# Weight halves at other places in their buffers, and two other orders of the queries' matmuls

## The chip, the cores and the metric

The kernel runs on one core of a Trainium2 chip. The metric is the device time of one execution in microseconds. A profiled execution has a span besides, from its first to its last instruction, and all positions below are microseconds from the start of that span.

## The reference, cut to what matters

Two decoder layers over 256 tokens of width 2048, in f32. The first is a Mamba-2 mixer: one wide projection of the modulated input, a causal convolution, a chunked scan, a gate, and a projection back. Then one shared K and V is made for three head groups of dilated attention, and the second layer attends with queries of its own.

```
h = x*(1+scale)+shift                      # modulation from c
z, xBC, dt = split(h @ in_w)               # 2048 x 10304
xBC = silu(causal_conv(xBC))               # xs (4096), B (1024), C (1024)
y = ssd_scan(xs*dt, dt*A, B, C) + D*xs;  y = rms(y*silu(z)) @ out_w
x = layer_norm(alpha*x + (1+gate)*y)
k, v = split(x @ kv_w)                     # 2048 x 6144, shared
q, z = split(h2 @ in_w2)                   # 2048 x 4096
o = merge(three dilated windows of softmax(q k) v) * silu(z)
out = layer_norm(alpha*x + (1+gate)*(o @ out_w2))
```

## The kernel before, in words

Nearly all work is matrix products with 256 tokens. Every f32 operand is held as two fp32r halves, a high half (`hi`, a rounded copy) and a low half (`lo`, the rest), and a product is made of hi by hi, hi by lo and lo by hi. A product is accumulated over 16 k-tiles of 128 rows of the contraction.

Weights come in pieces of 128 x 1024 f32 (512 KB). SyncE's queue loads each into `raw`; ScalarE copies it to `whi` (line 100), VectorE subtracts to get `wlo` (line 102). Both halves lie in buffers of 1088 elements per partition, four for each half, used in turn, so a piece of 1024 may start at any of the first 65 elements: `halves_at(off)` places hi at `off[0]` and lo at `off[1]`, in elements of 4 bytes. Two places are used: `SHORT = (16, 16)` and `LONG = (0, 0)`. The buffers themselves start at multiples of 256 bytes, and so does the activation tile `actT`.

There are three kinds of product:

- `tm_chunk` (lines 213 to 215): the activations are the loaded weights of TensorE (the stationary operand) and the weight halves stream past, 512 columns at a time. Their halves lie at LONG.
- `cm_quad` and `cm_piece` (lines 151 to 153): the weight halves are stationary, 128 x 128, and 256 columns of activations stream past. Their halves lie at SHORT. After the start of the kernel it makes the products for B and C, called `bc`, of groups 2, 4 and 6.
- `cm_wide` (lines 182 and 185), the wide products: the weight halves are stationary here too. For each k-tile four matmuls run: the two high halves (n = 0, 1) against 512 columns (activations hi and lo side by side, line 182), then the two low halves against 256 columns (activations hi, line 185). A call has 16 k-tiles in 4 pieces. There are 12 calls for xs (groups 2 to 7, two each, 256 to 483 us), 12 for K (766 to 899 us), 12 for the queries (two half sets `hq`, 965 to 1032 us, and 1034 to 1117 us among the first attention) and 4 for the second gate.

Below, a long matmul is one of 512 columns and a short one is one of 256 columns.

The order on TensorE follows the program's text nearly everywhere; the framework's scheduler interleaves the independent work of attention with the products. The next product's first piece is begun ahead (`begin_next`, `upcoming`), with the place given there by `firsts` or by the lists of the K products; this place has to be the same that the product itself uses.

Of the kernel before, what the change touches and what calls it, by code (L numbers as in the profile page):

```python
# [18 lines left out]
P = 128  # L19
L = 256  # L20
D = 2048
KT = D // P
# [5 lines left out]
NG = 3  # L28
# [21 lines left out]
def trunk(ctx, tc, xT, x, c, par, cst, bias, lnrow, ada, wdt, win, wxs, wout, wk, wv, wbin, wbout, out):  # L50
    nc = tc.nc
    V, S, T, PO = nc.vector, nc.scalar, nc.tensor, nc.gpsimd
# [27 lines left out]
    ones = cc[:, CM:CM + 128]  # L80
    cons.tile([P, 32], F32, name="pad")
    SHORT, LONG = (16, 16), (0, 0)

    def rows(t, b):

        return t.rearrange("(j r) n -> r j n", r=2)[b]
# [19 lines left out]
    upcoming, ready, owed = [], [], []  # L106
# [7 lines left out]
    def first_or(src, q, off=(0, 0)):  # L114

        return ready.pop() if ready else split(load_piece(src[q]), off=off)
# [38 lines left out]
    def acc_pair(pool=None):  # L155
        return [(pool or mm).tile([P, 2, L], F32, name="acc") for _ in range(2)]

    def cm_quad(src, ahi, alo, rate=(0, 1), k0=0):
        ps = acc_pair()
        for q in range(k0 // 2, KT // 2):  # L160
            w = first_or(src, q, SHORT)
            if q == KT // 2 - 1:
                begin_next()
            cm_piece(src, q, ps, ahi, alo, k0=k0, w=w)
            background(*rate)
        return ps

    def cm_wide(src, dst, rate=(0, 1), moving=None, later=False):

        both, high = moving or (lambda kt: xp[:, kt], lambda kt: xhi[:, kt, :])  # L170
        ps = acc_pair()
        for q in range(KT // 4):
            w = first_or(src, q, SHORT)
            if q == 1:
                settle()
            if q == KT // 4 - 1:
                begin_next()
            hi, lo = (t.rearrange("p k n -> p (k n)").rearrange("p (k n) -> p k n", k=4) for t in w)
            for k in range(4):
                kt = 4 * q + k  # L180
                for n in range(2):
                    T.matmul(ps[n], hi[:, k, n * P:n * P + P], both(kt), start=kt == 0, stop=False,  # L182
                             skip_group_check=True)
                for n in range(2):
                    T.matmul(ps[n][:, 0, :], lo[:, k, n * P:n * P + P], high(kt), start=False, stop=kt == KT - 1,  # L185
                             skip_group_check=True)
            background(*rate)
        def put():
            for n in range(2):
                S.activation(dst[:, n, :], ps[n][:, 1, :], AF.Copy)  # L190
                V.tensor_tensor(dst[:, n, :], ps[n][:, 0, :], dst[:, n, :], op=ALU.add)

        if later:
            owed.append(put)
        else:
            with behind_next():
                put()
# [125 lines left out]
    def drain():  # L323
        while jobs:
            jobs.pop(0)()


    hp = act.tile([P, 2, KT, L], F32R, name="actT")
    hhi, hlo = hp[:, 0], hp[:, 1]
# [4 lines left out]
    with ExitStack() as cA:  # L334
# [15 lines left out]
        with ExitStack() as cS:  # L350
# [8 lines left out]
            xs, bc, sz = {}, {}, dict(enumerate(szt))  # L359
# [29 lines left out]
            def xs_wide(g):  # L389

                xs[g] = pxs.tile([P, 4, L], F32, name="xs")
                for w in range(2):
                    t = xs[g][:, 2 * w:2 * w + 2, :]
                    cm_wide(wxs[2 * g - 4 + w], t, rate=R, moving=(lambda kt: hp[:, :, kt, :], hh_))
                    for n in range(2):
                        conv(t[:, n, :], 4 * g + 2 * w + n, t[:, n, :])

            def product(kind, g, pre=None):

                if kind == "xs" and g > 1:  # L400
                    return xs_wide(g)

                src, k0, part = begun.get((kind, g), (None, 0, None))
                if src is None:
                    src = win[{"bc": g // 2, "xs": 4 + g, "z": 6 + g}[kind]]
                if kind == "z":
                    ps = tm_chunk(src, hh_, hl_, rate=R, k0=k0, pre=pre)
                    if g not in sz:
                        sz[g] = p0.tile([P, 2, 512], F32, name="sz")
                    with behind_next():  # L410
                        for b in range(2):
                            if part is not None:
                                V.tensor_tensor(part[:, b, :], ps[b], part[:, b, :], op=ALU.add)
                            S.activation(sz[g][:, b, :], part[:, b, :] if part is not None else ps[b], AF.Silu)
                    return
                ps = cm_quad(src, hhi, hlo, rate=R, k0=k0)
                t = tiles(ps)
                if part is not None:
                    with behind_next():
                        for w in range(2):  # L420
                            V.tensor_tensor(part[:, 2 * w:2 * w + 2, :], ps[w], part[:, 2 * w:2 * w + 2, :],
                                            op=ALU.add)
                    t = [part[:, n, :] for n in range(4)]
                if kind == "xs":
                    xs_conv(g, t)
                else:
                    bc_conv(g, t)

            with ExitStack() as c0:
# [83 lines left out]
                for row in ("b4:0. b6:0. h z2:0. z1:0. b2:0 x1:0 h", "b2:1. x1:1. z1:1. z4:0 h h",  # L513
# [123 lines left out]
                for i, (k, q, ends) in enumerate(order):  # L637
# [7 lines left out]
                    for j in (i, i + 1):  # L645
                        if j < len(order) and j not in halves and order[j][0] != "dt":
                            with tc.issue_after(highs[j // 2 - 1]) if j in (7, 9) else ExitStack():
                                halves[j] = split(pieces[j], after=dots[0] if j == 5 else None,
                                                  off=LONG if str(order[j][0])[0] == "z" else SHORT)
# [5 lines left out]
                    z = str(k)[0] == "z"  # L655
# [3 lines left out]
                    k0, k1 = (begin[k], 2 * q + 2 if ends else KT) if k in part else (0, KT)  # L659
# [18 lines left out]
            aux2 = cS.enter_context(tc.tile_pool(name="aux2", bufs=2, space=PSUM, reuse_waits="tile"))  # L678
            px = pe = cS.enter_context(tc.tile_pool(name="px", bufs=2, reuse_waits="tile"))
            R = (1, 10)  # L680


            scratch = wp1.tile([P, D], F32, name="araw")
# [104 lines left out]

            def firsts(kind, g):
                if kind == "xs" and g > 1:  # L790
                    return [(wxs[2 * g - 4 + w], 0, SHORT) for w in range(2)]
                src, k0, _ = begun.get((kind, g), (None, 0, None))
                if src is None:
                    src = win[{"bc": g // 2, "xs": 4 + g, "z": 6 + g}[kind]]
                return [(src, k0 // 2, LONG if kind == "z" else SHORT)]

            for g in range(G - 1):
                for kind in ("bc",) * (g % 2) + ("xs", "z"):
# [108 lines left out]
        for n in range(4):  # L907
            ps = tm_chunk(wout[n], lambda kt: y_to(kt)[0], lambda kt: y_to(kt)[1],
                          nk=2 * KT, rate=(1, 4) if n else (1, 2),
                          pre={0: y_ahead, 3: first_weights}.get(n), split_end=4 if n == 3 else 0)  # L910
# [55 lines left out]
    kv, vt = {}, {}  # L966
# [11 lines left out]
    with ExitStack() as cL:  # L978
# [34 lines left out]
        for q in range(2, KT // 2):  # L1013
# [3 lines left out]
            for j in range(2):  # L1017
                with tc.issue_after(end.ins):
                    w = split(load_piece(wv[2 * j][q]), after=tile4.ins if q == 2 else None)
# [3 lines left out]

        R = (1, 2)
        pin[0] = latest[-1].ins
        with tc.issue_after(tile4.ins):
            state[0] = 0
            queue(pl, cols1[11:])
            jobs.append(lambda: gate_out(1))
            upcoming.extend((wk[2 * (2 * g + hq) + w], 0, SHORT) for hq in range(2) for g in range(NG) for w in range(2))  # L1030
            upcoming.extend((wv[1 + 2 * g], 0, LONG) for g in range(NG))
            evict_v(0, 2, tm_chunk(wv[4], hx, lx, rate=R))
            for hq in range(2):
                for g in range(NG):
                    kv[hq, g] = place(3 + 3 * hq + g, [P, 4, L])
                    for w in range(2):
                        cm_wide(wk[2 * (2 * g + hq) + w], kv[hq, g][:, 2 * w:2 * w + 2, :], rate=R, later=True)
            for g in range(NG):
                evict_v(1, g, tm_chunk(wv[1 + 2 * g], hx, lx, rate=R))
            drain()  # L1040
            late = latest[-1].ins

        ada_bias(1, slice(0, KT), slice(0, 2))
        for kt in range(KT):
            t = pl.tile([P, L], F32, name="htmp")
# [10 lines left out]
    R = (0, 1)  # L1056
# [22 lines left out]
    def queries(hq):  # L1079
        qq = [pc2.tile([P, 4, L], F32, name=f"q{g}") for g in range(NG)]  # L1080
        upcoming.extend([(wbin[2 * (2 * g + hq) + w], 0, SHORT) for g in range(NG) for w in range(2)][1:])
        for g in range(NG):
            for w in range(2):
                cm_wide(wbin[2 * (2 * g + hq) + w], qq[g][:, 2 * w:2 * w + 2, :], rate=(1, 1),
                        later=(g, w) != (NG - 1, 1))
        return qq

    def attend(hq, qq):
# [98 lines left out]
    for n in range(2):  # L1187
        ps = tm_chunk(wbout[n], *og, nk=H)
# [14 lines left out]
    ps = [tm_pair() for _ in range(2)]  # L1203
# [174 lines left out]
```

## Time and profile before

| what | value |
|---|---|
| time, median of 3 runs | 1234.39 us (1234.01 to 1234.89) |
| span of the profiled execution | 1233.4 us; no time of its own is listed for it beside the runs, so 1.0 us around the span is the median less the span |
| busy: TensorE matmul, weight load, VectorE, ScalarE | 99%, 85%, 83%, 57% |
| granted TensorE clock | 1.00 throughout |
| matmuls of lines 182 and 185 | 1280 and 1280 |

How to read it: busy TensorE time is a sum of modelled intervals that overlap, since the next matmul starts while the former drains. What a matmul costs in a dense stretch is therefore the distance between two starts, not the duration in a row. The timeline's rows give starts to 0.01 us, so the distance is taken over many rows. Rows of matmuls of the same line that follow one another are merged, with their count behind.

### The profile page before, as it was taken

What the parts mean: (1) busy time and instruction counts of PE and PEld (TensorE: products, weight loads), DVE (VectorE), ACT (ScalarE), POOL (GpSimd) and SP (SyncE); (2) the same over time, 40 slices, a digit from 0 to 9 for tenths busy, and PEclk for the clock granted to TensorE, in tenths of its full rate; (3) what the DMA queues carried; (4) which work ended last, traced back from release to release, by engine and by line L of the source; (5) the groups of instructions that cost most, each with busy time, mean ns of one, the idle gap of its engine ahead of it and who ended that gap; (6) DMA issues with size and microseconds to landing.
All of it is one profiled execution on the core that took longest, in us unless ns stands there. A gap on an engine that the chain in (4) does not pass through costs nothing.

```text
span 1233.4 us, 18854 instructions
## 1 busy us (share of the span) xinstructions
PE 1219.2 (99%) x7132; PEld 1048.7 (85%) x7132; DVE 1027.8 (83%) x1464; ACT 701.2 (57%) x1048; POOL 3.9 (0%) x8
## 2 busy tenths in 40 slices
PE   8999999999999999999999999999999999999998
PEld 7889988898888888888888788888888888888886
DVE  6999986999988989899768678888978866758776
ACT  4554477878597789764335544434445644445551
POOL 0000000000000000000000000000000000000001
PEclk9999999999999999999999999999999999999999
DMA  9999977687656556698998569989998774464673
GB/s 377 423 420 422 421 255 248 224 299 252 215 199 209 168 171 205 217 338 345 362 316 293 196 202 372 347 344 371 382 384 306 232 256 144 122 199 128 206 257 69
DMA packets 81371, 335.92 MB, mean 272 GB/s; under 512 B 9200, under 2 KB 9984, under 8 KB 68480
## 3 DMA queue, kind: packets, MB, share of 16 engines
q1 hardware_dynamic: 80352, 333.33, 75.0%
q0 software_dynamic: 576, 1.05, 0.6%
q8 instruction: 56, 0.92, 0.3%
q10 hardware_dynamic: 352, 0.34, 0.1%
q14 instruction: 35, 0.29, 0.1%
HBM read 331.45 MB, written 3.23 MB: 271 GB/s over the span
## 4 chain that ended last, share of the span: by engine, by line
PE 81%; DMA 10%; DVE 6%; ACT 2%; issue 1%; DVEq 0%; ACTq 0%; SPq 0%
PE acc L182 24%; PE acc L185 12%; PE acc L214 11%; PE acc L215 11%; PE acc L213 11%; DMA raw<-in_win 5%; DMA araw<-in_ada 3%; DVE wlo L102 2%; DVE araw L295 2%; PE py L776 1%; ACT whi L100 1%; PE acc L151 1%; PE acc L153 1%; PE acc L152 1%; PE acc L986 1%
## 5 line engine op out<-in xcount | busy, mean ns | idle before, releaser
L100 ACT ACTIVATE whi<-raw 128x1024 fp32r<-128x1024 f32 x389 | 408.5, 1058 | 358.7 <-PE acc L215 128.9
L102 DVE TENSOR_TENSOR wlo<-raw,whi 128x1024 fp32r<-128x1024 f32 x389 | 469.2, 1220 | 147.8 <-ACT whi L100 139.1
L182 PE MATMUL acc<-actT,whi 128*128 128x512 f32 x1280 | 402.7, 394 | 0.0
L185 PEld LDWEIGHTS acc<-actT,wlo 128*128 128x128 f32 x1280 | 239.6, 188 | 53.5 <-DVE wlo L102 0.5
L214 PE MATMUL acc<-wlo,actT 128*128 128x512 f32 x656 | 257.4, 392 | 2.8 <-DVE wlo L102 2.8
L185 PE MATMUL acc<-actT,wlo 128*128 128x256 f32 x1280 | 253.8, 280 | 0.0
L213 PE MATMUL acc<-whi,actT 128*128 128x512 f32 x656 | 253.5, 394 | 0.0
L295 DVE SCALAR_TENSOR_TENSOR araw<-araw,cb__72 128x2048 f32<-128x2048 f32 x95 | 217.0, 2284 | 2.9 <-DMA araw<-in_ada 2.6
L182 PEld LDWEIGHTS acc<-actT,whi 128*128 128x128 f32 x1280 | 193.9, 188 | 0.4
L215 PE MATMUL acc<-whi,actT 128*128 128x512 f32 x432 | 168.8, 391 | 0.0
L214 PEld LDWEIGHTS acc<-wlo,actT 128*128 128x128 f32 x656 | 123.2, 188 | 30.3 <-DVE wlo L102 5.1
L213 PEld LDWEIGHTS acc<-whi,actT 128*128 128x128 f32 x656 | 122.6, 188 | 24.2
L151 PE MATMUL acc<-actT,whi 128*128 128x256 f32 x372 | 103.1, 281 | 1.5 <-ACT actT L502 0.9
L153 PE MATMUL acc<-actT,wlo 128*128 128x256 f32 x372 | 101.9, 282 | 1.3 <-DVE wlo L102 1.1
L152 PE MATMUL acc<-actT,whi 128*128 128x256 f32 x372 | 103.1, 280 | 0.0
L215 PEld LDWEIGHTS acc<-whi,actT 128*128 128x128 f32 x432 | 81.1, 188 | 16.5
L215 PE MATMUL acc<-whi,ylo 128*128 128x512 f32 x224 | 87.6, 391 | 0.0
L151 PEld LDWEIGHTS acc<-actT,whi 128*128 128x128 f32 x372 | 69.6, 188 | 2.8 <-ACT actT L502 1.3
L153 PEld LDWEIGHTS acc<-actT,wlo 128*128 128x128 f32 x372 | 68.9, 188 | 2.5 <-DVE wlo L102 2.3
L152 PEld LDWEIGHTS acc<-actT,whi 128*128 128x128 f32 x372 | 70.6, 190 | 0.2
L215 PEld LDWEIGHTS acc<-whi,ylo 128*128 128x128 f32 x224 | 42.1, 188 | 8.5
L734 ACT ACTIVATE seg<-cbc,cumT 128x128 f32<-128x128 f32 x128 | 41.1, 389 | 3.5 <-PE py L776 2.1
(311 smaller groups left out, 1151.8 us busy)
## 6 DMA issues: line engine op xcount, KB each, us to landing
araw<-in_ada SPq DMA_DIRECT2D x96, 1024.0 KB, 7.2
raw<-in_win SPq DMA_DIRECT2D x109, 512.0 KB, 6.5
raw<-in_wout SPq DMA_DIRECT2D x64, 512.0 KB, 5.6
raw<-in_wbin SPq DMA_DIRECT2D x64, 512.0 KB, 3.8
raw<-in_wxs SPq DMA_DIRECT2D x48, 512.0 KB, 4.4
raw<-in_wv SPq DMA_DIRECT2D x48, 512.0 KB, 7.2
raw<-in_wk SPq DMA_DIRECT2D x48, 512.0 KB, 7.8
cbc<-cumd SPq DMA_DIRECT2D x16, 512.0 KB, 5.4
```

The lines of the kernel that those rows point to most:

```text
L100: copied.append(S.activation(hi, raw, AF.Copy))
L102: latest.append(V.tensor_tensor(lo, raw, hi.bitcast(F32), op=ALU.subtract))
L151: T.matmul(o, hi[:, k, c_], ahi[:, kt, :], start=first, stop=False, skip_group_check=True)
L152: T.matmul(o, hi[:, k, c_], alo[:, kt, :], start=False, stop=False, skip_group_check=True)
L153: T.matmul(o, lo[:, k, c_], ahi[:, kt, :], start=False, stop=kt == k1 - 1, skip_group_check=True)
L182: T.matmul(ps[n], hi[:, k, n * P:n * P + P], both(kt), start=kt == 0, stop=False, skip_group_check=True)
L185: T.matmul(ps[n][:, 0, :], lo[:, k, n * P:n * P + P], high(kt), start=False, stop=kt == KT - 1, skip_group_check=True)
L213: T.matmul(o, h_, hi[:, k, :], start=kt == k0, stop=False, skip_group_check=part)
L214: T.matmul(o, h_, lo[:, k, :], start=False, stop=False, skip_group_check=part)
L215: end = T.matmul(o, l_, hi[:, k, :], start=False, stop=kt == k1 - 1, skip_group_check=part)
L295: return V.scalar_tensor_tensor(raw, raw, 1.0, cb_, op0=ALU.mult, op1=ALU.mult, accum_out=mod[layer][:, ct, j:j + 1])
L734: S.activation(seg[:, hh, b, :], cbc[:, hh, b, :], AF.Relu, bias=cumT[:, b, h0 + hh:h0 + hh + 1], scale=-1.0)
```

## The change

The wide products of xs and of K take, product by product, one of twelve places from a table `PLACES`; the same twelve serve both. In elements the pairs (hi, lo) are (0,0), (32,32), (48,48), (8,8), (16,48), (48,16), (0,32), (32,0), (0,16), (16,0), (24,24), (16,32). The three `bc` products take (32,32), (48,48) and (32,48). The queries keep SHORT, but issue the four matmuls of a k-tile in another order: hi 0, lo 0, hi 1, lo 1 for the first half set, hi 0, hi 1, lo 1, lo 0 for the second. The second gate's products and all of `tm_chunk` stay. Nothing is added to or taken from the work of any engine or queue.

```diff
     SHORT, LONG = (16, 16), (0, 0)
+    PLACES = ((0, 0), (32, 32), (48, 48), (8, 8), (16, 48), (48, 16), (0, 32), (32, 0), (0, 16), (16, 0), (24, 24), (16, 32))
...
-    def cm_quad(src, ahi, alo, rate=(0, 1), k0=0):
+    def cm_quad(src, ahi, alo, rate=(0, 1), k0=0, off=SHORT):
...
-            w = first_or(src, q, SHORT)
+            w = first_or(src, q, off)
...
-    def cm_wide(src, dst, rate=(0, 1), moving=None, later=False):
+    def cm_wide(src, dst, rate=(0, 1), moving=None, later=False, off=SHORT, turn=(0, 1, 2, 3)):
...
-                for n in range(2):
-                    T.matmul(ps[n], hi[:, k, n * P:n * P + P], both(kt), start=kt == 0, stop=False,
-                             skip_group_check=True)
-                for n in range(2):
-                    T.matmul(ps[n][:, 0, :], lo[:, k, n * P:n * P + P], high(kt), start=False, stop=kt == KT - 1,
-                             skip_group_check=True)
+                for i in turn:
+                    n, half = i % 2, (hi, lo)[i // 2][:, k, i % 2 * P:i % 2 * P + P]
+                    T.matmul(ps[n] if i < 2 else ps[n][:, 0, :], half, (both if i < 2 else high)(kt),
+                             start=kt == 0 and i < 2,
+                             stop=kt == KT - 1 and i == [j for j in turn if j % 2 == n][-1], skip_group_check=True)
...
+                            off=PLACES[2 * g - 4 + w])        # xs, in xs_wide and in firsts
...
+                ps = cm_quad(src, hhi, hlo, rate=R, k0=k0, off=BC[g] if kind == "bc" else SHORT)
...
+            BC = {2: (32, 32), 4: (48, 48), 6: (32, 48)}
...
+                                off=PLACES[6 * hq + 2 * g + w])   # K, and in its upcoming list
...
-                        later=(g, w) != (NG - 1, 1))
+                        later=(g, w) != (NG - 1, 1), turn=(0, 1, 3, 2) if hq else (0, 2, 1, 3))
```

In the changed file `cm_wide` has one line, 184, for all four matmuls. The order on every engine is as before up to the queries. On TensorE, a k-tile in the middle of the first half set before (acc_9782 is the sum of n = 0, acc_9783 of n = 1; whi is a high half, wlo a low one):

```order
L182 MATMUL acc_9782<-actT_7030,whi_9803 128x512
L182 MATMUL acc_9783<-actT_7030,whi_9803 128x512
L185 MATMUL acc_9782<-actT_7030,wlo_9804 128x256
L185 MATMUL acc_9783<-actT_7030,wlo_9804 128x256
L182 MATMUL acc_9782<-actT_7030,whi_9803 128x512
```

and now, the same k-tile:

```order
L184 MATMUL acc_9782<-actT_7030,whi_9803 128x512
L184 MATMUL acc_9782<-actT_7030,wlo_9804 128x256
L184 MATMUL acc_9783<-actT_7030,whi_9803 128x512
L184 MATMUL acc_9783<-actT_7030,wlo_9804 128x256
L184 MATMUL acc_9782<-actT_7030,whi_9803 128x512
```

Long and short matmuls alternate now. On TensorE again, a k-tile of the second half set as it is now (acc_10554 is n = 0, acc_10555 is n = 1):

```order
L184 MATMUL acc_10554<-actT_7030,whi_10622 128x512
L184 MATMUL acc_10555<-actT_7030,whi_10622 128x512
L184 MATMUL acc_10555<-actT_7030,wlo_10623 128x256
L184 MATMUL acc_10554<-actT_7030,wlo_10623 128x256
L184 MATMUL acc_10554<-actT_7030,whi_10622 128x512
```

Here only the two short matmuls have changed places with each other; two long ones still come ahead of two short ones.

More of the change, by code (lines that the diff above doesn't have):

```diff
@@ L172, in cm_wide @@
         for q in range(KT // 4):
-            w = first_or(src, q, SHORT)
+            w = first_or(src, q, off)
             if q == 1:
@@ L393, in xs_wide @@
                     t = xs[g][:, 2 * w:2 * w + 2, :]
-                    cm_wide(wxs[2 * g - 4 + w], t, rate=R, moving=(lambda kt: hp[:, :, kt, :], hh_))
+                    cm_wide(wxs[2 * g - 4 + w], t, rate=R, moving=(lambda kt: hp[:, :, kt, :], hh_),
+                            off=PLACES[2 * g - 4 + w])
                     for n in range(2):
@@ L415, in product @@
                     return
-                ps = cm_quad(src, hhi, hlo, rate=R, k0=k0)
+                ps = cm_quad(src, hhi, hlo, rate=R, k0=k0, off=BC[g] if kind == "bc" else SHORT)
                 t = tiles(ps)
@@ L790, in firsts @@
                 if kind == "xs" and g > 1:
-                    return [(wxs[2 * g - 4 + w], 0, SHORT) for w in range(2)]
+                    return [(wxs[2 * g - 4 + w], 0, PLACES[2 * g - 4 + w]) for w in range(2)]
                 src, k0, _ = begun.get((kind, g), (None, 0, None))
@@ L794, in firsts @@
                     src = win[{"bc": g // 2, "xs": 4 + g, "z": 6 + g}[kind]]
-                return [(src, k0 // 2, LONG if kind == "z" else SHORT)]
+                return [(src, k0 // 2, LONG if kind == "z" else BC[g] if kind == "bc" else SHORT)]
             for g in range(G - 1):
@@ L1029, in trunk @@
             jobs.append(lambda: gate_out(1))
-            upcoming.extend((wk[2 * (2 * g + hq) + w], 0, SHORT) for hq in range(2) for g in range(NG) for w in range(2))
+            upcoming.extend((wk[2 * (2 * g + hq) + w], 0, PLACES[6 * hq + 2 * g + w])
+                            for hq in range(2) for g in range(NG) for w in range(2))
             upcoming.extend((wv[1 + 2 * g], 0, LONG) for g in range(NG))
@@ L1036, in trunk @@
                     for w in range(2):
-                        cm_wide(wk[2 * (2 * g + hq) + w], kv[hq, g][:, 2 * w:2 * w + 2, :], rate=R, later=True)
+                        cm_wide(wk[2 * (2 * g + hq) + w], kv[hq, g][:, 2 * w:2 * w + 2, :], rate=R, later=True,
+                                off=PLACES[6 * hq + 2 * g + w])
             for g in range(NG):
```

## The prediction

> **What bounds the kernel now.** I read the page first, its busy shares and its chain.
>
> ```profile
> span 1233.4 us, 18854 instructions
> PE 1219.2 (99%) x7132; PEld 1048.7 (85%) x7132; DVE 1027.8 (83%) x1464; ACT 701.2 (57%) x1048; POOL 3.9 (0%) x8
> PEclk9999999999999999999999999999999999999999
> PE 81%; DMA 10%; DVE 6%; ACT 2%; issue 1%; DVEq 0%; ACTq 0%; SPq 0%
> ```
>
> TensorE carries the end: 81% of the chain, busy 99% of the span, at full granted clock. The change touches only wide products, `bc` products and their weight halves, so the windows of these come next (columns: length, busy TensorE time and matmuls touched, granted clock, DMA share, GB/s). A window from a product's first start to the start behind its last counts one matmul or a few too many.
>
> ```profile
> 424.90:447.09 22.19, 22.19 (x131) 1.00 0.74 236
> 766.32:899.44 133.12, 133.12 (x769) 1.00 0.94 363
> 965.61:1032.37 66.76, 66.76 (x385) 1.00 0.76 244
> 1034.05:1117.06 83.01, 83.01 (x503) 1.00 0.51 156
> ```
>
> The first is two xs products: 32 k-tiles in 22.19 us, 693.4 ns each. The second is all twelve K products: 192 k-tiles in 133.12 us, 693.3 ns each. The third is the first half set of the queries: 96 k-tiles in 66.76 us, 695.4 ns each, a short stall at its start included. The fourth holds the second half set with the first attention among it. So a k-tile has one price, about 693.3 ns, wherever it runs undisturbed, and nothing but TensorE is waited for. Two rows of the page's groups say how little the halves are late over the whole run:
>
> ```profile
> L185 PEld LDWEIGHTS acc<-actT,wlo 128*128 128x128 f32 x1280 | 239.6, 188 | 53.5 <-DVE wlo L102 0.5
> ...
> L102 DVE TENSOR_TENSOR wlo<-raw,whi 128x1024 fp32r<-128x1024 f32 x389 | 469.2, 1220 | 147.8 <-ACT whi L100 139.1
> ```
>
> Of the loader's idle time before 1280 loads only 0.5 us is put down to VectorE, whose split of a full piece takes 1220 ns. Hence the question is only how fast TensorE streams, and the timeline of TensorE answers that, in K's stretch first:
>
> ```profile
> 801.00 0.62 PE L182 MATMUL acc<-actT,whi 128*128 128x512 f32 x2
> 801.47 0.39 PE L185 MATMUL acc<-actT,wlo 128*128 128x256 f32 x2
> 801.70 0.62 PE L182 MATMUL acc<-actT,whi 128*128 128x512 f32 x2
> 802.16 0.39 PE L185 MATMUL acc<-actT,wlo 128*128 128x256 f32 x2
> 802.39 0.62 PE L182 MATMUL acc<-actT,whi 128*128 128x512 f32 x2
> ```
>
> The two long ones take 0.46 to 0.47 us from start to start of the pair, the two short ones 0.23. Now the same shapes elsewhere: first and last row of 134 long matmuls of `tm_chunk`; of 100 short ones of `bc` 2 at 245 us; of 172 short ones of the first products at 113 us (all weights at SHORT in both); and of 46 short ones at the very end, whose stationary operand starts at a multiple of 256 bytes.
>
> ```profile
> 599.71 0.39 PE L213 MATMUL acc<-whi,actT 128*128 128x512 f32 x1
> ...
> 629.86 0.39 PE L214 MATMUL acc<-wlo,actT 128*128 128x512 f32 x1
> ...
> 244.74 0.28 PE L153 MATMUL acc<-actT,wlo 128*128 128x256 f32 x1
> ...
> 255.96 0.28 PE L153 MATMUL acc<-actT,wlo 128*128 128x256 f32 x1
> ...
> 112.78 0.28 PE L151 MATMUL acc<-actT,whi 128*128 128x256 f32 x1
> ...
> 132.92 0.28 PE L151 MATMUL acc<-actT,whi 128*128 128x256 f32 x1
> ...
> 1218.38 0.28 PE L215 MATMUL acc<-bs,s 128*128 128x256 f32 x1
> ...
> 1223.78 0.28 PE L215 MATMUL po<-whi,s 128*128 128x256 f32 x1
> ```
>
> That is 30.15/133 = 226.7 ns for a long one; 11.22/99 = 113.3 ns, 20.14/171 = 117.8 ns and 5.40/45 = 120.0 ns for a short one. So the same short matmul has three prices, held over long stretches, and the two at SHORT have the same code and the same places: what is held there is something like a phase, set when a stretch starts. The third price goes with another place of the stationary operand (and other moving tiles). A wide k-tile at the quick prices would be 2 x 226.7 + 2 x 113.3 = 680.0 ns; it takes 693.3, so 13.3 ns of it are slow steps.
>
> **The change part by part.** *Places of xs and K.* 24 products x 16 = 384 k-tiles change their place and nothing else. The writers of the halves keep their sizes, and VectorE and ScalarE aren't waited for. No row shows a wide product at another place. Lower end: all four matmuls quick, 680.0 ns, so 384 x -13.3 = -5.1 us. Upper end: the short ones at 120.0, and the long ones both at their slowest. The pair of long ones takes about 0.462 us of which the quick one is 0.227, so the slow one is about 0.236; then 2 x 236 + 2 x 120 = 712 ns and 384 x 18.7 = +7.2 us. Value: twelve places are twelve draws, and I have three states to draw from, 680.0, 693.3 and 712.0. With equal weight the mean is 695.1, so 384 x 1.8 = +0.7 us. I take equal weights because SHORT sits in the middle of the three.
>
> Here a rule of the Trainium skill stands against any effect. Its page "TensorE: Matmul & The Clock Gate", section "Step-by-step: what each phase is for", says that weight loads and the streamed operand have independent read ports of SBUF, and that loading the next tile's weights takes no read bandwidth from the running matmul. By it a place would cost nothing and this term would be 0 instead of +0.7 us. The trace fits it only in part: 113.3, 117.8 and 120.0 ns for one shape are not one port-bound rate, though no row here separates the place from the moving tiles.
>
> *Places of `bc`.* 144 + 48 + 48 = 240 short matmuls (the k-tiles left after what is begun early).
>
> ```profile
> 239.66:256.75 17.09, 17.09 (x149) 1.00 0.86 301
> 334.29:340.05 5.76, 5.76 (x51) 1.00 0.65 195
> 419.34:424.90 5.56, 5.56 (x51) 1.00 0.54 155
> ```
>
> Together 28.41 us, 118.4 ns each with their stalls. All quick would be 240 x 113.3 = 27.2, -1.2 us; all at 120.0 is 28.8, +0.4 us. Value -0.1 us, a draw at 117.8, the middle price.
>
> *Orders of the queries.* 12 products, 192 k-tiles, places unchanged. Ends as above per k-tile: 192 x -13.3 = -2.6 us and 192 x 18.7 = +3.6 us. The second order still has two long ones ahead of two short ones, all at SHORT; only the two low halves change places, whose starts differ by 512 bytes, and I give it 0. The first alternates long and short. In the stretch at 801 us one of the two long ones is quick and one slow, and the same holds for the short ones, so which of the two a matmul is goes by what ran before it and not by its kind; mixing them gives the same mean, 0. What it does ask for is each low half 227 ns earlier in a piece's first k-tile. That is covered: the loader waited 0.5 us for VectorE in the whole run. If the cover were gone, each of 24 pieces could wait 0.23 us, 5.5 us; a piece keeps TensorE for 2.77 us (4 x 693.3 ns) and its split VectorE for 1.22 us, so I don't expect it. The sums' eviction changes by a few hundred ns and has the next product's piece (2.77 us) as cover.
>
> *Sum.* +0.7 - 0.1 + 0 = +0.6 us on the profiled execution, span 1234.0; with the 1.0 us around it (median less span of before) 1235.0 us. That is 0.05% over the median of 1234.39. A measurement of this kernel tells about 0.2%, 2.5 us, from no change.
>
> **The rivals.** *Quick places (faster).* TensorE locks into the quick steps, as line 213 to 215 do for 30 us on end, at most of the twelve places. Price: -13.3 ns per k-tile; it decides from 186 of the 384 k-tiles on (2.5 us / 13.3 ns), that is when half of the places or more are quick and none slow. With eight of twelve, 256 k-tiles, -3.4 us: 1231.0. For it: 226.7 and 113.3 are the prices that the trace shows most steadily. Against: at SHORT none of the 12 K products reaches it, or their mean would be below 693.3, and the row at 120.0 is a place too. DMA is no hindrance: its share of 0.94 in K's stretch leaves room for the 1.9%.
>
> *Slow places (slower).* The short ones lock at 120.0 ns, as at the end of the kernel, at the places that are multiples of 256 bytes or off a 64-byte step, and take the long ones with them. Price up to +18.7 ns per k-tile; it decides from 134 k-tiles on, net of quick ones, so from a good third of the places. With half of the places, 192 k-tiles, +3.6 us: 1238.0.
>
> *No effect at all.* Places don't matter and the phase alone does; then xs, K and `bc` stay and 1234.4 comes out. For it: one and the same place has given 113.3 and 117.8 ns. Against: 120.0 ns comes only where the stationary operand lies elsewhere. It lies within 0.2% of my forecast and differs from it in its reason only. The Trainium skill's rule quoted above would give just this.
>
> *The new order waits for its low halves.* In the first half set, up to +5.5 us as worked out, 1239.9; against it speaks the 0.5 us.
>
> **How the numbers follow.** Draws that partly cancel, no effect included: 0.60 (0.40 for draws, 0.20 for no effect). Quick places: 0.17. Slow places: 0.20, a little more, since no row at all shows a place off the 64-byte step, and two of the twelve are. Waits of the new order: 0.03. So faster 0.17, same 0.60, slower 0.23. The likeliest case alone: three equally likely states of 680.0, 693.3 and 712.0 ns scatter by 13 ns, a place serves 32 k-tiles, so 0.42 us a place and 1.5 us for twelve; 1.3 times that is +-1.9 us, 1233.1 to 1236.9. The range that holds 8 in 10 takes in the rivals' usual sizes, 1231.3 to 1238.4: nearly down to eight quick places, and just past half the places slow. It leaves out the ends, -8.9 and +11.2 us, which are the sums of the bounds, and about 1 in 10 on either side.
>
> **What would show it.** In the changed profile each of the K products is a window of its own: 11.09 us now. Right: some at 10.88 (680.0 x 16), some longer, with a sum within 2.5 us of 133.12; the two halves of the queries within 1 us of 66.76 and 83.01. Wrong: all twelve moved to one side, which would mean that SHORT is an odd place and not a middle one; a first half set with idle time of the loader behind line 102; a distance of long starts beyond 236 ns, which no row here has and would break the upper end. Products of xs and K that share a place and differ in their time would say that the place isn't the cause.

## The result and the profile after

| | before | after |
|---|---|---|
| median | 1234.2 us (1233.9 to 1234.89, 4 runs) | 1239.54 us (1238.94 to 1240.44, 4 runs) |
| ratio after / before, 95% interval | | 1.0042 [1.0028, 1.0057] |
| profiled span | 1233.4 us | 1237.2 us (its own time 1238.94) |

The change made the kernel 0.42% slower. The prediction, 1235.0 us with a range up to 1238.4, was too low, and the result lies beyond its slower end. From the page of the kernel after: span, busy shares, and the row of the low halves' loads.

```profile
span 1237.2 us, 18851 instructions
PE 1224.2 (99%) x7132; PEld 1051.7 (85%) x7132; DVE 1028.2 (83%) x1464; ACT 702.2 (57%) x1048; POOL 3.9 (0%) x8
L184 PEld LDWEIGHTS acc<-actT,wlo 128*128 128x128 f32 x1280 | 239.4, 188 | 46.6 <-DVE wlo L103 0.4
```

Busy TensorE time grew by 5.0 us (1219.2 to 1224.2) with the same 7132 matmuls, and the loader waited 0.4 us for VectorE instead of 0.5. So the time went where the matmuls stream, not into a wait. Windows of TensorE after (length, busy time and matmuls touched, clock, DMA share, GB/s) show the stretches that the prediction had shown of before, at the same clock of 1.00: all twelve K products, the first half set of the queries, the second half set with the attention, and `bc` of groups 2, 4 and 6.

```profile
767.20:901.80 134.60, 134.60 (x769) 1.00 0.94 361
967.95:1035.97 68.02, 68.02 (x386) 1.00 0.77 240
1038.69:1120.90 82.21, 82.21 (x498) 1.00 0.52 154
238.99:256.74 17.75, 17.75 (x149) 1.00 0.86 302
...
419.94:425.66 5.72, 5.72 (x50) 1.00 0.54 160
```

K is 1.46 us longer (133.14 before; the prediction's window of 133.12 stops 0.02 us short of the last product's end), the first half set 1.26 us (66.76), `bc` 0.66, 0.00 and 0.16 us (17.09, 5.76, 5.56). The second half set's stretch is 0.80 us shorter, but it starts 2.72 us behind the first (1035.97 to 1038.69) where it was 1.67: attention matmuls changed sides of that start, a net +0.25 us. All of xs lies between 256 and 483 us: there the start of `xs` 0 came at 256.74 us (256.75 before) and the first K product at 767.20 (766.32), 0.88 us later, with two of the `bc` products in between (1.2 us later at 461 us, of which 0.3 was won back). The 0.66 us of `bc` 2 are not in this sum, since its stretch also began 0.67 us earlier (238.99 against 239.66). K's 1.46, the first half set's 1.26, this 0.88 and the 0.25 are 3.85 us; the span grew by 3.8.

Now K product by product: each row is a window from a product's first start to that of the next, in the order of the places in `PLACES`. First a row of before, then the twelve of after.

```profile
799.62:810.71 11.09, 11.09 (x66) 1.00 0.98 375
```

```profile
767.20:778.33 11.13, 11.13 (x65) 1.00 0.97 379
778.33:789.50 11.17, 11.17 (x66) 1.00 0.96 370
789.50:800.57 11.07, 11.07 (x66) 1.00 0.85 327
800.57:811.82 11.25, 11.25 (x66) 1.00 0.97 376
811.82:822.91 11.09, 11.09 (x66) 1.00 0.75 287
822.91:834.16 11.25, 11.25 (x66) 1.00 0.97 375
834.16:845.37 11.21, 11.21 (x67) 1.00 0.97 376
845.37:856.66 11.29, 11.29 (x66) 1.00 0.96 376
856.66:867.96 11.30, 11.30 (x66) 1.00 0.91 359
867.96:879.35 11.39, 11.39 (x66) 1.00 0.96 358
879.35:890.60 11.25, 11.25 (x66) 1.00 1.00 394
890.60:901.80 11.20, 11.20 (x66) 1.00 0.97 356
```

Divided by 16 k-tiles that is, in ns: (0,0) 695.6, (32,32) 698.1, (48,48) 691.9, (8,8) 703.1, (16,48) 693.1, (48,16) 703.1, (0,32) 700.6, (32,0) 705.6, (0,16) 706.2, (16,0) 711.9, (24,24) 703.1, (16,32) 700.0, against 693.3 at SHORT; windows are given to 0.01 us, so these hold to 0.6 ns. One place is better than SHORT, one equal, ten are worse. The xs products repeat this where nothing else runs among them: the same windows for (16,48) and (0,16) in xs.

```profile
340.21:351.30 11.09, 11.09 (x66) 1.00 0.56 175
425.66:436.96 11.30, 11.30 (x66) 1.00 0.72 225
```

11.09 and 11.30 us are K's figures for these places to the last digit, at another time and with another DMA share. So in this kernel the place carries the price. The timeline of TensorE in the first half set of the queries:

```profile
990.39 0.40 PE L184 MATMUL acc<-actT,whi 128*128 128x512 f32 x1
990.62 0.28 PE L184 MATMUL acc<-actT,wlo 128*128 128x256 f32 x1
990.74 0.40 PE L184 MATMUL acc<-actT,whi 128*128 128x512 f32 x1
...
992.15 0.40 PE L184 MATMUL acc<-actT,whi 128*128 128x512 f32 x1
```

Five pairs of long and short take 992.15 - 990.39 = 1.76 us, so two of them, a k-tile, take some 704 ns by these rows; over four products (979.43 to 1024.66, 45.23 us, 64 k-tiles) it is 706.7. Every long one is slow now (0.23 to 0.24 us to the short one behind it, where 226.7 ns is quick) and every short one too (0.12 us, where 113.3 ns is quick).

### The profile page after: what moved, and what is told of

It reads as the page before. It is cut to its first block, busy times and chain, and to the rows that moved or that the text cites. A ratio compares the mean times of both kernels' runs of the same rounds, so it can differ in the third digit from the quotient of the medians.

```text
span 1237.2 us, 18851 instructions
## 1 busy us (share of the span) xinstructions
PE 1224.2 (99%) x7132; PEld 1051.7 (85%) x7132; DVE 1028.2 (83%) x1464; ACT 702.2 (57%) x1048; POOL 3.9 (0%) x8
## 4 chain that ended last, share of the span: by engine, by line
PE 82%; DMA 10%; DVE 5%; ACT 2%; issue 1%; SPq 0%; ACTq 0%; DVEq 0%
PE acc L184 36%; PE acc L214 11%; PE acc L215 11%; PE acc L213 11%; DMA raw<-in_win 5%; DMA araw<-in_ada 3%; DVE araw L295 2%; DVE wlo L103 2%; PE py L778 1%; DMA raw<-in_wv 1%; PE acc L152 1%; PE acc L154 1%; PE acc L153 1%; ACT whi L101 1%; PE acc L988 1%
## 5 line engine op out<-in xcount | busy, mean ns | idle before, releaser
L184 PE MATMUL acc<-actT,whi 128*128 128x512 f32 x1280 | 412.0, 396 | 0.0
L184 PE MATMUL acc<-actT,wlo 128*128 128x256 f32 x1280 | 271.4, 281 | 0.0
L184 PEld LDWEIGHTS acc<-actT,whi 128*128 128x128 f32 x1280 | 202.9, 188 | 9.2
L154 PE MATMUL acc<-actT,wlo 128*128 128x256 f32 x372 | 102.1, 282 | 1.2 <-DVE wlo L103 0.9
L152 PEld LDWEIGHTS acc<-actT,whi 128*128 128x128 f32 x372 | 69.6, 188 | 3.3 <-ACT s L636 1.5
L153 PEld LDWEIGHTS acc<-actT,whi 128*128 128x128 f32 x372 | 70.6, 190 | 0.2
```

The source lines that it names most:

```text
L152: T.matmul(o, hi[:, k, c_], ahi[:, kt, :], start=first, stop=False, skip_group_check=True)
L153: T.matmul(o, hi[:, k, c_], alo[:, kt, :], start=False, stop=False, skip_group_check=True)
L154: T.matmul(o, lo[:, k, c_], ahi[:, kt, :], start=False, stop=kt == k1 - 1, skip_group_check=True)
L184: T.matmul(ps[n] if i < 2 else ps[n][:, 0, :], half, (both if i < 2 else high)(kt), start=kt == 0 and i < 2, stop=kt == KT - 1 and i == [j ...
```

## The experiments

Theories that stood against each other. *Place*: a wide k-tile has a price that goes by where its two halves lie. *Distance*: what counts isn't the place itself but how far it is from the place of the moving operand. *Place and order*: the price goes by which weights are loaded under which matmul, so the same place has another price in another order. *State*: TensorE keeps a pace that a stretch's start or a disturbance sets, and the place only decides which paces can last. And *mishap*: a start of attention or a wait carries the loss. Runs that were timed have a ratio to the kernel before on the same chip.

**Only the places.** The change without the queries' orders:

```diff
-                        later=(g, w) != (NG - 1, 1), turn=(0, 1, 3, 2) if hq else (0, 2, 1, 3))
+                        later=(g, w) != (NG - 1, 1))
```

> Only the places of xs, K and bc are those of the change; the queries issue their matmuls in the order of before. Theory P (each pair of places has a price per k-tile of its own, and the prices add up): the twelve K products take 134.6 us as in the changed kernel, the xs products some 1.4 us more than before, both halves of the queries 693.3 ns per k-tile; the span is 2.6 to 3.2 us over that of before. Theory O (the new order of the queries, with what it moves among the first attention, costs most): within 1 us of before. If the two parts do not add up, the sum of this and of the order alone is not the 5.3 us of the change.

1237.83 us (1236.83 to 1238.83, 11 runs), ratio 1.0024 [1.0015, 1.0033], span 1235.5, that is 2.1 us over before by the profiles, a little under the 2.6 expected, and 2.83 us by the medians (1235.0 before on this chip). Windows of all K products and of the first half set:

```profile
766.92:901.53 134.61, 134.61 (x769) 1.00 0.93 360
967.68:1034.43 66.75, 66.75 (x385) 1.00 0.79 244
```

K takes what it takes in the whole change, 134.61 us against 134.60, and the queries are as in before. Place by place the windows of K repeat to 0.01 us. TensorE is busy through the whole of K's window, so *mishap* falls for K.

**Only the orders.** All places SHORT:

```diff
-    PLACES = ((0, 0), (32, 32), (48, 48), (8, 8), (16, 48), (48, 16), (0, 32), (32, 0), (0, 16), (16, 0), (24, 24), (16, 32))
+    PLACES = (SHORT,) * 12
...
-            BC = {2: (32, 32), 4: (48, 48), 6: (32, 48)}
+            BC = {2: SHORT, 4: SHORT, 6: SHORT}
```

> Only the two orders of the queries; all places as before. Theory P: xs and K at 693.3 ns per k-tile, the first half set of the queries at 706.7 (+1.3 us), the second at 693.3; the span 1.0 to 1.5 us over before. Theory O: 3 us or more over before.

1235.59 us (1234.9 to 1238.96, 11 runs), ratio 1.0008 [0.9999, 1.0017], span 1234.9. The same two windows, and one of four products in the middle of the first half set, here and in before:

```profile
766.37:899.48 133.11, 133.11 (x769) 1.00 0.93 361
965.66:1033.67 68.01, 68.01 (x385) 1.00 0.74 240
977.14:1022.37 45.23, 45.23 (x259) 1.00 0.77 256
```

```profile
976.90:1021.28 44.38, 44.38 (x259) 1.00 0.78 261
```

K stays, the first half set loses 1.25 us: 45.23/64 = 706.7 ns per k-tile against 44.38/64 = 693.4. The second order costs nothing; its undisturbed products stay at 693.3. The time itself can't be told from before, but the two parts' ratios, 1.0024 and 1.0008, make 1.0032 together, inside both intervals of the whole change (the other one follows).

**The change again**, timed in more rounds.

> The changed kernel itself once more, beside the kernel before and on the same chip as the runs sent with it. If places and orders add up, 1.0032 of before (1.0024 for the places and 1.0008 for the orders): about 3.4 to 4.2 us over it. If they do not add up, 5 us or more, as in its first runs.

1239.62 us (1239.49 to 1239.83, 5 runs), ratio 1.0039 [1.0026, 1.0052], span 1237.7, with the same windows at each place to 0.01 us.

**Moving operand 64 bytes further.** A gap of 64 bytes is put between the weight buffers and the activation tile, which is the moving operand of the wide products and the stationary one of `tm_chunk`; all else is the change. It moves whatever lies behind it too.

```diff
+    gap = ctx.enter_context(tc.tile_pool(name="gap", bufs=1))
+    gap.tile([P, 16], F32, name="gap")
```

> The changed kernel with 64 bytes left free between the weight buffers and the activation tile, so that the activations and all that lies behind them move by 64 bytes and the weight halves stay. If the absolute place of the stationary halves sets the price, K stays as in the changed kernel: 696, 698, 692, 703, 693, 703, 700, 706, 706, 711, 703, 700 ns per k-tile in the order of the table, and the second half set of the queries 693.3. If the place relative to the moving tile does, each pair costs what the pair that is 16 elements lower on both sides costs: (32,32) 693, (48,48) 698, (16,48) 700, (48,16) 706, (0,32) 703, (32,0) 693, (16,32) 706, (0,0) 692 to 698, and the second half set of the queries, at (16,16), 696 to 698. In the long matmuls of lines 213 to 215 the activations are the stationary operand: by the first reading their 226.7 ns changes too, by the second it need only change because the two tiles have moved apart.

1250.3 us in its one run, span 1248.5. K's windows at (0,0) and (32,32), then (16,32) in its xs product and in its K product:

```profile
776.72:787.76 11.04, 11.04 (x66) 1.00 0.94 358
787.76:798.85 11.09, 11.09 (x66) 1.00 1.00 380
...
476.60:487.91 11.31, 11.31 (x67) 1.00 0.64 204
899.68:910.88 11.20, 11.20 (x67) 1.00 0.97 362
```

With the gap, a place lies where the place less 16 elements lay before, seen from the activations, modulo 64 elements. (32,32) now takes 11.09 us, the figure of (16,16) before; (0,0) takes 11.04, near the 11.07 of (48,48); (0,32) takes 11.25 (843.78 to 855.03 us), that of (48,16); (32,0) takes 11.11, near the 11.09 of (16,48). Ten places have such a counterpart, nine of the table and SHORT in the second half set (696.6 ns per k-tile now, near the 695.6 of (0,0)). Nine of the ten agree with it within 2.2 ns per k-tile. The tenth is (16,32), which should have had the 706 of (0,16): its K product had 700.0 (11.20 us), but its xs product 706.9 (11.31 us), the price expected. The same holds of (0,16) in this run, 705.6 in xs and 700.0 in K. So *distance* holds in the main, *place* alone falls, and two places show two paces each. Most of the loss is elsewhere, though. The same stretch of 574 long matmuls of `tm_chunk`, where the activations are stationary, in the change and with the gap:

```profile
567.00:696.91 129.91, 129.91 (x575) 1.00 0.87 318
```

```profile
571.27:704.96 133.69, 133.69 (x574) 1.00 0.85 308
```

129.91/573 = 226.7 ns has become 133.69/573 = 233.3. A second stretch, 116 such matmuls, went the same way, from 26.37 us (930.33 to 956.70) to 27.06 (940.01 to 967.07). The product whose halves nobody had moved had been at a quick distance and lost it. This is one run of one gap, and all tiles behind the gap moved with it.

**The alternating order at all places.** xs, K and the gate alternate long and short (K and xs at the twelve places), the first half set has the old order at six further places.

```diff
-    def cm_wide(src, dst, rate=(0, 1), moving=None, later=False, off=SHORT, turn=(0, 1, 2, 3)):
+    def cm_wide(src, dst, rate=(0, 1), moving=None, later=False, off=SHORT, turn=(0, 2, 1, 3)):
```

> All wide products of xs, K and the second gate issue hi 0, lo 0, hi 1, lo 1; xs and K at the twelve places of the change. The first half set of the queries goes back to two long ones ahead of two short ones and takes six further pairs of places: (0,48), (48,0), (32,16), (32,48), (48,32), (40,40). If the alternating order is slow by itself, every K product takes about 706.7 ns per k-tile whatever its place, and the gate's undisturbed products 706.7. If order and place act together, K spreads as widely as in the changed kernel (692 to 711), with another ranking, and some pair may go below 693. The six further pairs: those whose two places differ by 16 elements or 48 near 700 to 711, (40,40) near 700 as (8,8) and (24,24), 703.

1239.36 us in its one run, span 1237.6. SHORT, now in the gate, again takes 706.6 ns per k-tile. The other places have changed rank: (48,16) has 693.6 (703.1 in the old order), (0,32) 697.4 (700.6), (0,16) 694.1 (706.2), but (0,0) 705.6 (695.6) and (48,48) 706.6 (691.9). But in this run xs and K don't agree at every place: (0,0) has 694.4 in xs (257.56 to 268.67 us) against the 705.6 in K, (16,32) has 700.0 against 705.6, so K's ranking is in part one of paces. None of the six further places in the old order is below SHORT's 693.3 (some 694 to 707); (0,48) and (48,0), at 694 and 699, lie under the 700 that was expected. And the worst place of the old order, (16,0), is the best of all; the timeline inside its xs product:

```profile
439.89 0.39 PE L185 MATMUL acc<-actT,whi 128*128 128x512 f32 x1
...
440.91 0.39 PE L185 MATMUL acc<-actT,whi 128*128 128x512 f32 x1
```

Three pairs in 1.02 us, 680 ns per k-tile: all four matmuls quick. Its K product began so and lost it in its middle, at 874.77 us, behind one k-tile that the scheduler had issued as long, long, short, short. The same kind of k-tile made the K product at (0,32) quicker: 5.61 us for the eight k-tiles ahead of it (701 ns each), 4.85 for the seven behind (693). So *place and order* holds, and *state* is needed besides.

**All forty wide products at (16,0), alternating**, once with that order left to the scheduler, once held by dependencies between the four matmuls of a k-tile:

```diff
+    WIDE = (16, 0)
+    PLACES = (WIDE,) * 12
...
+                    with tc.issue_after(mark[0].ins) if i != turn[0] else ExitStack():   # held order only
+                        mark[0] = T.matmul(...)
```

> The same with the order left to the scheduler, which puts two long matmuls together in 9 of the 640 k-tiles, one of them at the start of each of several K and query products. Theory L with a memory of the phase: behind such a k-tile the product falls to about 700 ns per k-tile, as the tenth K product did from its middle on in the run with the alternating order (680.0 ahead of it), and stays there up to the next disturbance; 1 to 4 us over the pinned version. If the order of one k-tile does not matter, the two are equal.

> All 40 wide products at (16, 0) with the alternating order hi 0, lo 0, hi 1, lo 1, kept fixed within each k-tile; bc at (16, 16) as before. Theory L: the price of a matmul hangs on where the weights lie that are loaded while it streams, relative to its moving operand; under a long one a distance of 0 is quick (as in lines 213 to 215), under a short one 64 bytes. In this version every long one has a low half at 0 loaded beneath it and every short one a high half at 64 bytes, so K, xs, the queries and the gate take 680.0 ns per k-tile wherever attention does not break in: 34 products x 16 x -13.3 ns = -7.3 us, 1227 to 1229 against 1235.0, ratio 0.994 to 0.995. The rival, that 680.0 at (16, 0) was luck of one stretch's start, gives some products at 680 and the rest near 700: 1231 to 1238.

Left to the scheduler: 1235.32 us (1233.5 to 1236.62, 10 runs), ratio 1.0006 [0.9997, 1.0016]. Held: 1233.09 us (1229.74 to 1234.68, 11 runs), ratio 0.9983 [0.9974, 0.9992]. The timeline of the version left to the scheduler around 826 us, and its windows of K ahead of that and behind it, and of four products of the first half set:

```profile
825.88 0.62 PE L185 MATMUL acc<-actT,whi 128*128 128x512 f32 x2
826.34 0.40 PE L185 MATMUL acc<-actT,wlo 128*128 128x256 f32 x2
826.57 0.40 PE L185 MATMUL acc<-actT,whi 128*128 128x512 f32 x1
```

```profile
809.56:820.44 10.88, 10.88 (x67) 1.00 0.79 300
831.47:887.44 55.97, 55.97 (x323) 1.00 0.97 377
976.26:1021.49 45.23, 45.23 (x258) 1.00 0.80 257
```

At 825.88 two long ones run in a row; ahead of that a product takes 10.88 us (680.0 ns per k-tile), and the five products behind it 55.97/80 = 699.6. That one k-tile takes 0.69 us (825.88 to 826.57), 0.01 more than a quick one; what it costs is the pace behind it. The scheduler reordered the ninth k-tile of each K product from there on, so each stretch of slow pace between two such k-tiles is 15 k-tiles, some 10 us; none of them brought the quick pace back. In the first half set only the first k-tile is out of order, and the four products shown, behind it, take 45.23/64 = 706.7. With the order held, all of K stays quick and the queries' first half set too, but not the second. Windows: ten K products, an xs product, four products of the first half set, three of the second.

```profile
776.34:885.14 108.80, 108.80 (x643) 1.00 0.96 370
423.04:434.24 11.20, 11.20 (x67) 1.00 0.68 221
973.47:1016.99 43.52, 43.52 (x259) 1.00 0.82 268
1068.40:1102.00 33.60, 33.60 (x194) 1.00 0.63 188
```

108.80/160 and 43.52/64 are both 680.0 ns, while an xs product at 423 us and three products of the second half set take 700.0, with the same code at the same place. Other xs products of this execution, at 256 and 391 us, take 10.88 us, 680.0 ns per k-tile. So the theory of 680.0 throughout (1227 to 1229 us) failed and its rival was right: the place allows both paces. That what ran before decides is what the timeline at 826 us shows for one case; for the others it is inferred. Runs of this kernel spread over 4.9 us, those of the kernel before beside it over 2.4 and those of the change over 0.3; only the run of 1230.33 us was profiled, so that this spread is the same thing is an inference too.

**Places around (16,0)**, one for each product of xs and K, order held: (12,0), (20,0), (8,0), (24,0), (16,4), (16,8), (40,0), (48,0), (16,60), (16,56), (18,0), (14,0).

> Alternating order, pinned; xs and K at twelve places around (16, 0): (12,0), (20,0), (8,0), (24,0), (16,4), (16,8), (40,0), (48,0), (16,60), (16,56), (18,0), (14,0); queries and gate at (16, 0). If only whole steps of 64 bytes count, (12,0) to (18,0) differ little and (48,0) is the slow one. If the quick state is narrow, only places within a few elements reach 680 and the rest lie at 693 to 711. The queries' first half set stays at 680.0 in either case.

1236.35 us in its one run. With the high half moved by two elements, 8 bytes, no product reached 680: (18,0) has 693.6 in K and (14,0) 706.2. (16,4) had 693.6 in K and 680.4 in xs, and (48,0), 128 bytes away, 681.6 and 700.1, so neither of the two readings expected fits. The first half set at (16,0) stayed at 680.0, as expected. Only (16,60) was quick both times; its xs and its K product:

```profile
424.59:435.47 10.88, 10.88 (x66) 1.00 0.72 221
856.62:867.50 10.88, 10.88 (x66) 1.00 0.95 371
```

**A mixed version and all at (16,60).** The mixed one keeps SHORT and the old order where the quick pace had not lasted (xs and the second half set) and has (16,0), alternating and held, for K, the first half set and the gate. The other has all forty at (16,60), held.

```diff
-    WIDE = (16, 0)
+    WIDE = (16, 60)
```

> Products of xs, the gate's undisturbed ones at SHORT where the before had them and the second half set of queries as in before (SHORT, the four matmuls as long, long, short, short); the twelve products of K, the first half set of queries and the gate's products at (16, 0) with long and short in turn, that order held by waits. Theory that place and order together set the price: xs 693.3 ns per k-tile, K 680.0, first half set 680.0, second half set 693.3. Against before K gains 12 x 16 x 13.3 ns = 2.56 us and the first half set 6 x 16 x 13.3 = 1.28 us; a ratio near 0.997 and a median near 1231. Rival that a stretch can start in either of two states whatever its place (680 or 700 at (16, 0)): K or the first half set at 700 in some runs, medians spread over 1229 to 1236 and a ratio of 0.998 to 1.000. Rival that the price is in the place alone: the same as in the run with all products at (16, 0).

> All forty wide products at (16, 60), long and short in turn, that order held by waits. In the run with a place for each product near (16, 0), this place was quick in both of its products (680.0 ns per k-tile). Theory that this place is quick whatever came before it: xs, K, both half sets and the gate's undisturbed products at 680 ns per k-tile, which against 693.3 is 13.3 ns x 16 x 36 products = 7.7 us less than before, 1227. Rival that two states last there as at (16, 0), and the stretch's start decides: some stretches at 700, the time between 1229 and 1236 and different from run to run.

The mixed one: 1231.11 us (1229.97 to 1232.92, 8 runs), ratio 0.9975 [0.9965, 0.9986]. All at (16,60): 1230.04 us (1229.13 to 1230.76, 5 runs), ratio 0.9963 [0.9951, 0.9976], the lowest median of this study, ahead of both kernels; its interval overlaps the mixed one's. Windows of the mixed one, ten K products, three of the second half set and one of the gate; then the gate's product in the version with all at (16,0), held:

```profile
776.51:885.31 108.80, 108.80 (x643) 1.00 0.95 367
1068.57:1101.85 33.28, 33.28 (x195) 1.00 0.64 190
1153.16:1164.36 11.20, 11.20 (x67) 1.00 0.63 197
```

```profile
1153.40:1164.28 10.88, 10.88 (x67) 1.00 0.69 207
```

680.0 and 33.28/48 = 693.3 ns per k-tile, as *place and order* had it, and the time is the 1231 expected. But the gate, at (16,0) in the same held order, takes 700.0 here and 680.0 in the other version: *state* is at work in the mixed one too. Windows of the version at (16,60): an xs product and three products of the second half set.

```profile
422.67:433.98 11.31, 11.31 (x66) 1.00 0.74 221
1067.95:1101.23 33.28, 33.28 (x194) 1.00 0.65 189
```

That is 706.9 and 693.3 ns per k-tile, and four products of the first half set take 43.52 us, 680.0, all at one place in one order. (16,60) too has paces that last, three of them here, so the expectation of 680 throughout (1227) failed and the one of states held. All twelve K products and the first half set were quick in both versions' profiles.

## Why the prediction was wrong

- *What bounds the kernel*: right. TensorE's pace carried all of it; no wait came in, and the rival of low halves that come late didn't happen (0.4 us of waits).
- *Places of xs and K*, +0.7 us: the direction was right and the size was not. K measured +1.46 us, and the stretch with xs and two `bc` products +0.88. Per k-tile the draws were put at a mean of 695.1 ns; K's mean is 134.60/192 = 701.0. The step that failed is the sentence "I take equal weights because SHORT sits in the middle of the three": 680.0, 693.3 and 712 were taken as equally likely. The twelve draws had none at 680, one below 693.3, and one at 711.9; SHORT is near the good end of its order, so another place mostly loses. The 712 was itself worked out from short matmuls with other tiles, at 120.0 ns. The slowest place, (16,0), came to it (711.9), and in its middle went past it: three k-tiles take 872.22 - 870.08 = 2.14 us, 713.3 each, with 0.24 to 0.25 us for a pair of short ones where the upper end had 0.24.
- *The first order*, 0: the failed sentence is that "which of the two a matmul is goes by what ran before it and not by its kind; mixing them gives the same mean". Mixing gave 706.7, all four slow, +1.26 us by the window and +1.25 in the run of the orders alone. It had been read off one order, in which a long one behind a short one takes 226 ns by the trace's starts; in the new order a long one behind a short one takes 235. So what ran just before doesn't decide alone, and there is no mean that mixing keeps. The second order's 0 was right.
- *Places of `bc`*, -0.1 us: measured +0.66, 0.00 and +0.16 us, +0.8 in all, beyond the upper end of +0.4 (only the 0.16 is inside the 0.88 above). That end took 120.0 ns and left the stalls at nothing. The value compared 117.8 ns with 118.4, a figure that holds stalls; the prediction's own row has `bc` 2 at 113.3 ns, the quick price, so there it had nothing to gain.
- *The 1.0 us around the span* came from a profile and a median of different executions. After, the profiled execution has 1238.94 - 1237.2 = 1.74 us, so 0.7 us of the miss of 4.5 is level and not the change. Another 0.6 is the profiled run against the median (1238.94 and 1239.54); the remaining 3.2 is the span, +3.8 where +0.6 was forecast.
- *The rivals*: "slow places" has the right direction; ten of the twelve were slower. Its condition fits in part: (8,8) and (24,24), off the 64-byte step, have 703.1, but (0,0), a multiple of 256 bytes on both sides, only 695.6, and (48,16), neither, 703.1. That its 1238.0 lies near the result is partly luck, since the first order's 1.26 us and the level are not in it. "No effect at all" falls: the places alone give 1.0024 [1.0015, 1.0033]. The Trainium skill's page "TensorE: Matmul & The Clock Gate", section "Step-by-step: what each phase is for", has loads of the next weights take no read bandwidth from the running matmul. What the prediction drew from it, that a place costs nothing, isn't borne out: K's products differ by 0.32 us (11.07 to 11.39) in nothing but where the weights lie. That it is the loads that slow the stream is not shown by this, though; the recorded load has a mean of 188 ns before and after.
- *What would show it*: products of xs and K that share a place agree in this kernel, though not in the runs with the gap and with the alternating order. K's sum stayed within 2.5 us, but no product came to 10.88 us, and the first half set missed its 1 us. "All twelve moved to one side" nearly came true, and its reading, SHORT as an odd place, with it.

What is shown is that places and orders carry the loss: the places by their own run's time and windows, the first order by its window. What stays open is why a distance is quick or slow, and what, apart from a k-tile out of order, throws a stretch from one pace to another.

## What to carry to other kernels

Where TensorE streams without a wait, the start addresses of both operands are a tuning knob of some per cent of the stream (680 to 712 ns for one k-tile here), and it has to be set for place and order together, not one after the other: the worst place of one order was, when its quick pace held, the best of the other. Before other places are drawn at random, ask where the present one ranks: it need not be a middle. And a quick pace has to be protected, by an order that the scheduler can't change within a tile (0.9983 against 1.0006 here), and looked for product by product in the windows.

## What the hardware showed unexpectedly

- A step of 64 bytes of a tile that the change doesn't touch took 226.7 ns long matmuls to 233.3, 3.8 us over one stretch of 574.
- The pace has a memory: at (16,0), alternating, 680.0 and 700.0 ns per k-tile lasted in one execution for 108.8 and for 33.6 us on end, and one reordered k-tile changed it for the k-tiles behind it.
- The paces that came again and again, 680.0, 693.3, 700.0 and 706.7 ns per k-tile, are 102, 104, 105 and 106 times 6.667 ns. Figures between them, as the 703.1 of (8,8), are means over 16 k-tiles that differ among themselves.
